# Up-projection's partial sums formed in PSUM: products 6, 7 and 4 added onto product 1, with the pipeline over feature pairs

## The chip, the cores and the metric

One core of one Trainium2 chip runs the whole program in one launch. The core has a matrix engine (PE, TensorE), which multiplies a stationary 128 x 128 weight tile with a moving operand and writes, or adds, the product to an accumulator memory (PSUM, 8 banks of 512 float32 columns over 128 partitions); a vector engine (DVE, VectorE); a scalar engine (ACT, ScalarE); a third one, GpSimd (POOL); and a queue (SP) that issues transfers between the chip's memory and the on-chip buffers. Each engine works through its own list of instructions in order; semaphores make one wait for another. The metric is the time of one execution on the device in microseconds (us), as the median of several runs.

## What is computed

One layer of an encoder: chunked attention and an mLSTM memory side by side, an output projection, and then the feed-forward part, which alone the change touches:

```python
def conv_ffn(h, buf, w_up, w_conv, b_conv, w_down):
    S = h.shape[1]
    u = h @ w_up
    ext = jnp.concatenate([buf.astype(u.dtype), u], axis=1)
    y = b_conv
    for j in range(CONV_W):
        y = y + ext[:, j:j + S] * w_conv[j]
    gate, up = jnp.split(y, 2, axis=-1)
    out = (jax.nn.gelu(gate, approximate=True) * up) @ w_down
    return out, ext[:, S:]
```

There are 2048 prompt tokens and 8 x 16 sample tokens, each of width 1024. `w_up` has 2 x 2816 columns: 2816 for the gate and 2816 for the value `up`; everything is in float32.

## The kernel before

The feed-forward part runs over three blocks of tokens (`FBLOCKS`; 768, 768 and 640 columns). For each block there is an up-projection over 22 features of 128 gate and 128 value columns each, and then a down-projection in two halves. In the profile the up-projections lie at about 1315 to 1645, 1838 to 2150 and 2350 to 2620 us.

**Seven products instead of eight.** For a feature the four results (gate and value, for either half of the block's columns) are a 2 x 2 block product over two halves of the depth, done with seven products in Winograd's form. The moving operands, the seven combinations of the tokens, are `B0` to `B6`, kept in the buffers and made before the block; the weights' sums s1 to s4 are formed on DVE in block 0 (`load_quads`, L1275), stored (`wsd`) and read back in blocks 1 and 2. Each product (`product`) is 12 matmuls into one bank: 4 steps of depth by three terms of a float32 number that is split in a high and a low part (`mm3`, L95 high by high, L96 high by low, L97 low by high). `HALF` is the number of columns of one: 384, 384 and 320. The split of a weight tile takes an ACT cast (L1258) and a DVE subtraction (L1259); seven 128 x 512 tiles a feature.

**The chain of sums.** In the order P1, P6, P7, P5, P2, P4, P3:
- P1 goes to bank `a` (`ua`, from the PSUM tag mm); ACT copies it to x1 (L1481).
- P6 goes to `ub` (tag sm); DVE forms x2 = x1 + P6 (L1483).
- P7 goes to `e`, the first half of `uec` (tag big); DVE forms x3 = x2 + P7 (L1485).
- P5 goes to `c`, the second half of `uec`; DVE adds x3 and c to the second half of the value, uu (`second`, L1411).
- P2 is added onto `a`, and ACT copies it as the first half of the gate, ug (L1498); P4 is added onto `e`, and DVE forms the first half of uu as x2 + e (L1500); P3 is added onto `c`, and DVE adds x2 and c to the second half of ug (L1411).

The profile's buffer names drop numbers, so x1 to x3 all read `x`. Each tag of PSUM has two tiles. x1 to x3 share three slots.

**What follows for a feature.** `conv`: two halo copies on POOL, one ACT step (L1430) and two DVE steps (L1431, L1432) for uu and for ug each, the gelu on ACT (L1434), the product of both on DVE (L1506), and a store to `gd`.

**What sets the order.** `pend` holds the weights two groups ahead (`ahead_of`); a group is the first four (g = 0) or the last three (g = 1) weight tiles of a feature. Split tiles lie in turn in a pair `wh`/`wl` or in four tiles w3. The order in which an engine's instructions stand is set when the program is built: a scheduler simulates the program as written and sorts each engine's queue by it, so that the matmuls of one feature stand among those of its neighbours. On the chip this order is fixed, and each engine waits at its next instruction.

Of the kernel before, what the change touches and what calls it, by code (L numbers as in the profile page):

```python
# [44 lines left out]
def hymba_step(ctx: ExitStack, tc: tile.TileContext, I: dict, O: dict):  # L45
# [981 lines left out]
    P1, P6, P7, P5, P2, P4, P3 = range(7)  # L1027
# [233 lines left out]
    raws = {}  # L1261

    def load_quads(b, f, g):

        src = lambda i: I["w_up"][f][:, i * 512:(i + 1) * 512]
        if b == 0 and g == 0:
            q = []
            for i in range(4):
                q.append(quad(f"wu{f}_{i}"))
                nc.sync.dma_start(q[i], src(i))  # L1270
            a11, a12, a22, a21 = q
            s1, s2, s3, s4 = [quad(f"ws{f}_{i}") for i in range(4)]
            for o, x, y, op in ((s1, a21, a22, ALU.add), (s2, s1, a11, ALU.subtract), (s3, a11, a21, ALU.subtract),
                                (s4, a12, s2, ALU.subtract)):
                nc.vector.tensor_tensor(o, x, y, op=op)  # L1275
            for i, o in enumerate((s2, s3, s1, s4)):
                nc.sync.dma_start(wsd[f][:, i * 512:(i + 1) * 512], o)
            raws[f] = [a12, a22, s4]
            return [a11, s2, s3, s1]
        if b == 0:  # L1280
            return raws.pop(f)
        kept = lambda i: wsd[f][:, i * 512:(i + 1) * 512]
        out = []
        for i, s_ in enumerate([[src(0), kept(0), kept(1), kept(2)], [src(1), src(2), kept(3)]][g]):
            r = quad(f"wu{b}_{f}_{g}_{i}")
            nc.sync.dma_start(r, s_)
            out.append(r)
        return out

    def load_up(b, f, g, quads=None):  # L1290
# [9 lines left out]
        for (h, l), r in zip(at, quads or load_quads(b, f, g)):  # L1300
            split(h, l, r)
        return at
# [73 lines left out]
    p4 = ffn.p4 = ctx.enter_context(tc.tile_pool(name="p4", bufs=1, side="right", reuse_waits="tile"))  # L1376
    pend = [load_up(0, 0, 0)]
# [17 lines left out]
    for b, tiles in enumerate(FBLOCKS):  # L1395
# [70 lines left out]

        def w3_tile(name):
            return p4.tile([P, 1056], F32R, tag="w3", name=name, bufs=4)

        for f in range(NF):  # L1470
# [10 lines left out]
            nc.scalar.copy(x1[:, :n], a[:, :n])  # L1481
# [3 lines left out]
            nc.vector.tensor_tensor(x3[:, :n], x2[:, :n], e[:, :n], op=ALU.add)  # L1485
            product(P5, w[3], c)
# [30 lines left out]
        for dh in range(2):  # L1517
# [7 lines left out]
            if dh == 1:  # L1525
                order = order[2:] + order[:2]
            for c in range(6):
# [5 lines left out]
                elif not last:  # L1533
                    quads = [load_quads(b + 1, 0, i) for i in range(2)]
                    pend = [load_up(b + 1, 0, 0, quads[0])]
# [151 lines left out]
```

## Time and profile before

| what | value |
|---|---|
| time, median of 3 runs | 2800.45 us (2796.61 to 2802.93) |
| profiled execution | 2790.47 us, its span 2788.7 us |
| PE busy | 2725.1 us (98%) |
| DVE busy | 1877.9 us (67%) |
| ACT busy | 1407.6 us (50%) |
| up-projection, block 0: DVE busy in 300 us from 1340 us | 277.8 us |
| up-projection, block 1: DVE busy in 240 us from 1880 us | 190.4 us |

The profile is one execution of its own, so its span is compared with its own time and not with the median. Engines overlap; busy times don't add up to the span. A group of the profile is all instructions of one line, engine, operation and tile, with the mean duration of one. Matmuls overlap in the pipeline: their pace is the distance of two starts and less than the duration of one. In rows of a timeline the first number is the start, the second the duration; what stands in brackets is the engine's idle time before and who ended it.

### The profile page before, as it was taken

To read this page: it belongs to the slowest core of one execution; us is meant where nothing else is said; L and a number is where in the kernel's file an instruction comes from. 1 tells how busy PE (TensorE), PEld (TensorE's weight loads), DVE (VectorE), ACT (ScalarE), POOL (GpSimd) and SP (SyncE) were. 2 spreads that over 40 slices of the span, in tenths; PEclk is the share of its full clock that TensorE was granted. 3 is DMA by queue.
4 is the path that set the end of the run, shared out by engine and by line. 5 is a ranking of instruction groups with operands and counts; after the bars stand their busy time and mean duration, and the time that the engine had idled before them with its cause. 6 is when DMAs were issued, how large, how long until landed. Compare 5 with 4: busy or idle time off the path is not lost.

```text
span 2788.7 us, 47032 instructions
## 1 busy us (share of the span) xinstructions
PE 2725.1 (98%) x16587; PEld 2549.4 (91%) x16587; DVE 1877.9 (67%) x3442; ACT 1407.6 (50%) x2836; POOL 429.0 (15%) x876
## 2 busy tenths in 40 slices
PE   8899999999999999999999999999999999999998
PEld 7899999998899998888999988899999878999887
DVE  5344455656546678666999986468778854888855
ACT  4345545644356666544554555345445543555443
POOL 1000010212100003244211110011111211222211
PEclk9999999999999999999999999999999999999999
DMA  4544355547555455356555455644444774555585
GB/s 165 174 128 126 111 152 160 178 152 219 166 173 148 144 180 172 104 175 227 190 174 167 168 172 174 221 142 156 152 153 151 269 268 146 177 178 175 197 300 188
DMA packets 313418, 486.04 MB, mean 174 GB/s; under 512 B 55426, under 2 KB 150622, under 8 KB 313054
## 3 DMA queue, kind: packets, MB, share of 16 engines
q1 hardware_dynamic: 274590, 449.21, 50.0%
q10 hardware_dynamic: 38592, 33.83, 3.6%
q8 instruction: 130, 2.13, 0.3%
q14 instruction: 106, 0.87, 0.1%
HBM read 359.36 MB, written 126.70 MB: 174 GB/s over the span
## 4 chain that ended last, share of the span: by engine, by line
PE 54%; DVE 3%; DMA 1%; issue 1%; POOL 1%; ACT 1%; SPq 0%; DVEq 0%; POOLq 0%; ACTq 0%
PE uec L95 6%; PE uec L96 6%; PE uec L97 6%; PE dn L97 4%; PE dn L96 3%; PE dn L95 3%; PE ua L97 3%; PE ua L96 3%; PE ua L95 3%; PE dnm L97 2%; PE dnm L95 2%; PE dnm L96 2%; PE wo L97 2%; PE wo L95 2%; PE wo L96 2%; PE ub L97 1%
## 5 line engine op out<-in xcount | busy, mean ns | idle before, releaser
L95 PE MATMUL uec<-B,wuh 128*128 128x384 f32 (+1 forms) x720 | 235.3, 328 | 1.0 <-DVE uu L1411 0.7
L96 PE MATMUL uec<-B,wuh 128*128 128x384 f32 (+1 forms) x720 | 235.4, 327 | 0.0
L97 PE MATMUL uec<-B,wul 128*128 128x384 f32 (+1 forms) x720 | 234.2, 327 | 0.0
L1259 DVE TENSOR_TENSOR gl<-gr,gh 128x768 fp32r<-128x768 f32 (+3 forms) x141 | 121.4, 871 | 153.3 <-ACT gh L1258 137.4
L1258 ACT CAST gh<-gr 128x768 fp32r<-128x768 f32 (+3 forms) x141 | 102.0, 735 | 198.9 <-PE dn L96 174.4
L1258 ACT CAST wuh<-wu 128x512 fp32r<-128x512 f32 x255 | 141.7, 618 | 112.4 <-PE uec L96 100.4
L95 PE MATMUL dn<-wdh,gh 128*128 128x512 f32 x466 | 183.1, 393 | 2.0 <-DVE ug L1411 2.0
L96 PE MATMUL dn<-wdl,gh 128*128 128x512 f32 x466 | 184.0, 395 | 0.0
L97 PE MATMUL dn<-wdh,gl 128*128 128x512 f32 x466 | 168.2, 396 | 0.0
L1259 DVE TENSOR_TENSOR wul<-wu,wuh 128x512 fp32r<-128x512 f32 x255 | 164.9, 685 | 2.8 <-DMA x2d<-mx 2.8
L96 PE MATMUL vo<-wi_l,hT 128*128 128x256 f32 x544 | 155.9, 287 | 0.0
L95 PE MATMUL vo<-wi_h,hT 128*128 128x256 f32 x544 | 155.2, 285 | 0.6 <-DVE mt L199 0.6
L97 PE MATMUL vo<-wi_h,hT 128*128 128x256 f32 x544 | 155.5, 286 | 0.0
L387 DVE CUSTOM_DVE_ANT_0 tmp<-s,nb 128x640 f32<-128x640 f32 (+4 forms) x128 | 94.4, 737 | 80.6 <-PE s L377 74.7
L95 PEld LDWEIGHTS uec<-B,wuh 128*128 128x128 f32 x720 | 135.2, 188 | 3.3 <-DVE uu L1411 1.2
L96 PEld LDWEIGHTS uec<-B,wuh 128*128 128x128 f32 x720 | 135.5, 188 | 0.2
L97 PEld LDWEIGHTS uec<-B,wul 128*128 128x128 f32 x720 | 135.4, 188 | 0.0
L388 ACT ACTIVATE tmp<-tmp,mn 128x640 f32<-128x640 f32 (+4 forms) x128 | 97.6, 762 | 69.5 <-DVE mn L387 65.9
L95 PE MATMUL qk<-hT,wi_h 128*128 128x384 f32 (+1 forms) x384 | 128.4, 334 | 2.9 <-ACT qk_st L226 1.2
L400 DVE TENSOR_TENSOR ptl<-pt,pth 128x640 fp32r<-128x640 f32 (+4 forms) x128 | 93.6, 738 | 55.5 <-ACT pth L399 54.6
L97 PE MATMUL qk<-hT,wi_l 128*128 128x384 f32 (+1 forms) x384 | 128.1, 333 | 0.0
L96 PE MATMUL qk<-hT,wi_h 128*128 128x384 f32 (+1 forms) x384 | 127.8, 333 | 0.0
(411 smaller groups left out, 8875.8 us busy)
## 6 DMA issues: line engine op xcount, KB each, us to landing
wu<-in_w_up SPq DMA_DIRECT2D x220, 256.0 KB, 3.9
wu<-wsd SPq DMA_DIRECT2D x176, 256.0 KB, 3.7
wdr<-in_w_down SPq DMA_DIRECT2D x132, 256.0 KB, 5.0
gr<-gd SPq DMA_DIRECT2D x78, 384.0 KB, 3.1
wi_raw<-in_w_in SPq DMA_DIRECT2D x52, 512.0 KB, 4.0
wsd<-ws SPq DMA_DIRECT2D x88, 256.0 KB, 2.8
gd<-g SPq DMA_DIRECT2D x44, 384.0 KB, 2.4
kraw<-kTd SPq DMA_DIRECT2D x112, 128.0 KB, 3.3
```

What stands on the lines that cost most here:

```text
L95: nc.tensor.matmul(out, ah, bh, start=start, stop=False, skip_group_check=onto)
L96: nc.tensor.matmul(out, ah, bl, start=False, stop=False, skip_group_check=onto)
L97: nc.tensor.matmul(out, al, bh, start=False, stop=stop, skip_group_check=onto)
L387: nc.vector.tensor_tensor_reduce(o_, s_, b_, 1.0, 3e38, ALU.add, ALU.min, accum_out=mn)
L388: nc.scalar.activation(tmp[:, :n], tmp[:, :n], AF.Exp, bias=mn, scale=-1.0, accum_out=rsum[:, i % 4, hh:hh + 1])
L400: nc.vector.tensor_tensor(s.ptl[:, sl, qc], ptv, s.pth[:, sl, qc], op=ALU.subtract)
L1258: nc.scalar.copy(h, r)
L1259: nc.vector.tensor_tensor(l, r, h, op=ALU.subtract)
```

## The change

The seven products are made in the order P1, P5, P6, P2, P7, P4, P3. P6, P7 and P4 are added onto P1 in the same bank `ua`, and ACT copies the running sum out after each: x1 (L1497 or L1520 of the changed kernel), x2 (L1502), x3 (L1507) and the first half of uu (L1522). P5 and then P3 go to `uc` (tag big, one half of it used), P2 to `ud` (tag sm), where DVE adds x1 to it (L1505). `second` is L1424, the convolution L1443 to L1447, the product of gate and value L1528. Three of the five DVE additions of a feature stay, and two ACT copies become four.

P1 of the next feature is issued in this feature's turn, before P4; its weight tile (a11) is therefore loaded (`load_first`) and split with the group before, as the first of g = 1, and the very first of a block on its own (`split_first`). The weights' sums of block 0 are stored in another order, and `late_B` fills the operands of P2, P7, P4 and P3. The rotation of the down-projection's order at dh == 1 is dropped.

```diff
-    P1, P6, P7, P5, P2, P4, P3 = range(7)
+    P1, P5, P6, P2, P7, P4, P3 = range(7)
...
-        for i in (P5, P2, P4, P3):
+        for i in (P2, P7, P4, P3):
...
+    def load_first(b, f):
+
+        firsts[f] = quad(f"wf{b}_{f}")
+        nc.sync.dma_start(firsts[f], I["w_up"][f][:, 0:512])
+        return firsts[f]
...
+        if g:
+            first = [load_first(b, f + 1)] if f < NF - 1 else []
+            return first + (raws.pop(f) if b == 0 else fetched(src(2), kept(3)))
+        if b:
+            return fetched(kept(0), kept(1), src(1), kept(2))
+        a11 = firsts.pop(f)
+        a21, a22, a12 = fetched(src(3), src(2), src(1))
...
+        for i, o in enumerate((s1, s2, s3, s4)):
+            nc.sync.dma_start(wsd[f][:, i * 512:(i + 1) * 512], o)
+        raws[f] = [a22, s4]
+        return [s1, s2, a12, s3]
...
+    def split_first(b, quad_):
+        t = p4.tile([P, 1056], F32R, tag="w3", name=f"wuf{b}", bufs=4)
+        split(t[:, 0:512], t[:, 512:1024], quad_)
+        return t[:, 0:512], t[:, 512:1024]
...
-            a, d_, ec = ps_mm(f"ua{nm}"), ps_sm(f"ub{nm}"), ps_big(f"uec{nm}")
-            e, c = ec[:, 0:512], ec[:, 512:1024]
-            x1, x2, x3 = [p4.tile([P, 384], F32, tag="x", name=f"x{i}_{nm}", bufs=3) for i in range(3)]
-            product(P1, w[0], a)
-            nc.scalar.copy(x1[:, :n], a[:, :n])
-            product(P6, w[1], d_)
-            nc.vector.tensor_tensor(x2[:, :n], x1[:, :n], d_[:, :n], op=ALU.add)
-            product(P7, w[2], e)
-            nc.vector.tensor_tensor(x3[:, :n], x2[:, :n], e[:, :n], op=ALU.add)
-            product(P5, w[3], c)
+            nxt = f"{b}_{f + 1}"
+            if f == 0:
+                a, x1 = ps_mm(f"ua{nm}"), x_tile(f"x1_{nm}")
+                product(P1, first, a)
+                nc.scalar.copy(x1[:, :n], a[:, :n])
+            c, d_, e = ps_big(f"uc{nm}")[:, 0:512], ps_sm(f"ud{nm}"), a
+            product(P5, w[0], c)
+            product(P6, w[1], e, onto=True)
+            x2, x3 = x_tile(f"x2_{nm}"), x_tile(f"x3_{nm}")
+            nc.scalar.copy(x2[:, :n], e[:, :n])
+            product(P2, w[2], d_)
+            ug = u_tile(f"ug{nm}")
+            nc.vector.tensor_tensor(ug[:, 2:2 + n], x1[:, :n], d_[:, :n], op=ALU.add)
+            product(P7, w[3], e, onto=True)
+            nc.scalar.copy(x3[:, :n], e[:, :n])
             uu = u_tile(f"uu{nm}")
             second(uu, x3, c)
             w = pend.pop(0)
...
-            ug = u_tile(f"ug{nm}")
-            product(P2, w[0], a, onto=True)
-            nc.scalar.copy(ug[:, 2:2 + n], a[:, :n])
-            product(P4, w[1], e, onto=True)
-            nc.vector.tensor_tensor(uu[:, 2:2 + n], x2[:, :n], e[:, :n], op=ALU.add)
-            product(P3, w[2], c, onto=True)
+            else:
+                a, x1 = ps_mm(f"ua{nxt}"), x_tile(f"x1_{nxt}")
+                product(P1, w.pop(0), a)
+                nc.scalar.copy(x1[:, :n], a[:, :n])
+            product(P4, w[0], e, onto=True)
+            nc.scalar.copy(uu[:, 2:2 + n], e[:, :n])
+            product(P3, w[1], c, onto=True)
             second(ug, x2, c)
...
             order = list(range(nt))
-            if dh == 1:
-                order = order[2:] + order[:2]
...
+            if dh:
+                first = split_first(b + 1, quads[0])
```

How the queues read with it is shown at two places. In the names the first number is the block, the second the feature, and the last a running number; `B` is numbered by the position of its product in the order. First PE in block 1, feature 4, before: the end of P7 (`B2`), and what comes next, P2 of the same feature (`B4`) and P3 of feature 3 (`B6`).

```order
L95 MATMUL uec1_4_21825<-B2_1_19737,wu31_4_0_1_21657 128x384
L96 MATMUL uec1_4_21825<-B2_1_19737,wu31_4_0_1_21657 128x384
L97 MATMUL uec1_4_21825<-B2_1_19737,wu31_4_0_3_21659 128x384
L95 MATMUL ua1_4_21823<-B4_1_19739,wuh1_4_1_21735 128x384
L96 MATMUL ua1_4_21823<-B4_1_19739,wuh1_4_1_21735 128x384
L97 MATMUL ua1_4_21823<-B4_1_19739,wul1_4_1_21736 128x384
L95 MATMUL uec1_3_21678<-B6_1_19741,wuh1_3_1_21586 128x384
L96 MATMUL uec1_3_21678<-B6_1_19741,wuh1_3_1_21586 128x384
L97 MATMUL uec1_3_21678<-B6_1_19741,wul1_3_1_21587 128x384
```

The products after P7 go to other tiles than the one P7 wrote. PE at the same place of the changed kernel: the end of P7 (now `B4`) and the start of P4 (`B5`).

```order
L95 MATMUL ua1_4_21769<-B4_1_19740,wu31_4_0_1_21678 128x384
L96 MATMUL ua1_4_21769<-B4_1_19740,wu31_4_0_1_21678 128x384
L97 MATMUL ua1_4_21769<-B4_1_19740,wu31_4_0_3_21680 128x384
L95 MATMUL ua1_4_21769<-B5_1_19741,wuh1_4_1_21755 128x384
L96 MATMUL ua1_4_21769<-B5_1_19741,wuh1_4_1_21755 128x384
L97 MATMUL ua1_4_21769<-B5_1_19741,wul1_4_1_21756 128x384
```

P4 now stands directly behind P7, in the same bank, and the copy of x3 has to be made between the two. ACT around that copy, block 1, feature 4 of the changed kernel:

```order
L1502 COPY x2_1_4_21870<-ua1_4_21769 128x384
L1447 ACTIVATE y1_3_0_21818<-y1_3_0_21818 128x768
L1258 CAST wu31_5_1_1_21903<-wu1_5_1_1_21909 128x512
L1507 COPY x3_1_4_21871<-ua1_4_21769 128x384
L1520 COPY x1_1_5_21919<-ua1_5_21918 128x384
L1522 COPY uu1_4_21900<-ua1_4_21769 128x384
```

Between the copies of x2 and x3 stand the gelu of feature 3 and a cast of a weight tile for feature 5, whose slot P7 of feature 4 has read. The same place in block 0, feature 10, where the gelu stands behind the cast:

```order
L1502 COPY x2_0_10_17861<-ua0_10_17750 128x384
L1443 ACTIVATE y0_9_0_17799<-ug0_9_17723,wcv_16243 128x768
L1258 CAST wu30_11_1_1_17894<-ws11_3_17818 128x512
L1447 ACTIVATE y0_9_0_17799<-y0_9_0_17799 128x768
L1507 COPY x3_0_10_17862<-ua0_10_17750 128x384
```

Before, ACT had two copies a feature there, of x1 and of ug, and no copy of P7's bank.

More of the change, by code (lines that the diff above doesn't have):

```diff
@@ L1259, in split @@
         nc.vector.tensor_tensor(l, r, h, op=ALU.subtract)
-    raws = {}
+    raws, firsts = {}, {}
+    def load_first(b, f):
+        firsts[f] = quad(f"wf{b}_{f}")
+        nc.sync.dma_start(firsts[f], I["w_up"][f][:, 0:512])
+        return firsts[f]
     def load_quads(b, f, g):
         src = lambda i: I["w_up"][f][:, i * 512:(i + 1) * 512]
[L1266 to L1281, printed above, removed]
-        kept = lambda i: wsd[f][:, i * 512:(i + 1) * 512]
[L1283 to L1288, printed above, removed]
@@ new lines, in load_quads, with fetched @@
+        kept = lambda i: wsd[f][:, i * 512:(i + 1) * 512]
+        def fetched(*srcs):
+            out = [quad(f"wu{b}_{f}_{g}_{i}") for i in range(len(srcs))]
+            for o, s_ in zip(out, srcs):
+                nc.sync.dma_start(o, s_)
+            return out
+        if g:
[3 more added lines that the diff above has]
+            return fetched(kept(0), kept(1), src(1), kept(2))
@@ L1376, in hymba_step @@
     p4 = ffn.p4 = ctx.enter_context(tc.tile_pool(name="p4", bufs=1, side="right", reuse_waits="tile"))
+    first = split_first(0, load_first(0, 0))
     pend = [load_up(0, 0, 0)]
@@ L1465, in split_g, with x_tile @@
             parts[dh, k] = gh, gl
+        def x_tile(name):
+            return p4.tile([P, 384], F32, tag="x", name=name, bufs=3)
         def w3_tile(name):
@@ L1533, in hymba_step @@
                 elif not last:
-                    quads = [load_quads(b + 1, 0, i) for i in range(2)]
-                    pend = [load_up(b + 1, 0, 0, quads[0])]
+                    quads = [load_first(b + 1, 0)] + [load_quads(b + 1, 0, i) for i in range(2)]
+                    pend = [load_up(b + 1, 0, 0, quads[1])]
                 ks = list(range(4 * c, 4 * c + (4 if c < 5 else 2)))
@@ L1591, in hymba_step @@
                 pass
-            pend.append(load_up(b + 1, 0, 1, quads[1]))
+            pend.append(load_up(b + 1, 0, 1, quads[2]))
     nc.sync.dma_start(O["conv_prompt"], halo)
```

9 lines of the change are left out of this document (7 added, 2 removed).

## The prediction

> **What bounds the kernel now.** I read the page first: the busy times, then the 40 slices.
>
> ```profile
> span 2788.7 us, 47032 instructions
> PE 2725.1 (98%) x16587; PEld 2549.4 (91%) x16587; DVE 1877.9 (67%) x3442; ACT 1407.6 (50%) x2836; POOL 429.0 (15%) x876
> ...
> PEclk9999999999999999999999999999999999999999
> ```
>
> TensorE (PE) is busy for 98% of the span at the full granted clock. The change leaves the number of matmuls in the up-projection as it is, so it can only move the time by PE's idle time. The second view is the table by windows, for the three up-projections (block 0 about 1315 to 1645 us, block 1 about 1838 to 2150, block 2 about 2350 to 2620). Its columns are the window, its length, then busy time and count for PE, PEld, DVE, ACT and POOL, the clock, the DMA share and GB/s.
>
> ```profile
> 1340.00:1400.00 60.00, 58.55 (x335) 57.94 (x334) 55.10 (x86) 30.25 (x48) 15.01 (x16) 1.00 0.62 195
> 1400.00:1460.00 60.00, 59.87 (x344) 59.55 (x343) 56.23 (x88) 30.38 (x51) 10.26 (x16) 1.00 0.50 167
> 1460.00:1520.00 60.00, 59.62 (x339) 58.69 (x339) 54.40 (x84) 30.58 (x49) 9.90 (x16) 1.00 0.50 167
> 1520.00:1580.00 60.00, 59.33 (x340) 58.90 (x340) 55.85 (x85) 29.09 (x47) 11.59 (x16) 1.00 0.52 173
> 1580.00:1640.00 60.00, 59.84 (x344) 59.53 (x343) 56.24 (x88) 32.35 (x53) 10.07 (x18) 1.00 0.50 165
> ...
> 1940.00:2000.00 60.00, 60.00 (x346) 60.00 (x345) 46.86 (x70) 29.50 (x47) 6.98 (x16) 1.00 0.49 155
> ...
> 2480.00:2540.00 60.00, 60.00 (x412) 60.00 (x411) 54.07 (x110) 34.49 (x60) 13.39 (x40) 1.00 0.55 177
> ```
>
> Blocks 1 and 2 have no PE idle time at all; nothing can be won there. Block 0 has a little: VectorE (DVE) is busy 93% of the time there (277.8 of 300 us), since it also forms the weight sums, and PE loses 2.8 us by its busy time, or, against some 346.8 matmuls per window at block 1's pace, 32 matmuls of 0.173 us = 5.5 us. **So the most that the change can win here is 5.5 us, and it can lose wherever PE now waits.**
>
> **What the change adds: a read between two products of one bank.** Before, P1 goes to `ua`, P6 to `ub`, P7 to half of `uec`, and nothing accumulates onto P6 or P7 until their sums have long been read. Now P6, P7 and P4 go onto P1's bank, and each partial sum is copied out by ACT before the next product may start. Where the other feature's products stand between, the copy is free. The order of the changed kernel shows where they do not: in every third feature (4, 7, ..., 19 of each block, 18 places) P4 follows P7 directly, and in feature 0 of block 2. The price of such a place comes from these rows of block 1: the last two matmuls of P1 and the next product's first, the copy that waits for P1, and a wait of PE for a DVE split.
>
> ```profile
> 1907.31 0.34 PE L96 MATMUL ua<-B,wuh 128*128 128x384 f32 x1
> ...
> 1907.48 0.34 PE L97 MATMUL ua<-B,wul 128*128 128x384 f32 x1
> ...
> 1907.65 0.34 PE L97 MATMUL ub<-B,wul 128*128 128x384 f32 x1
> ...
> 1907.85 0.48 ACT L1481 COPY x<-ua 128x384 f32<-128x384 f32 x1 [2.00 <-PE ua L97]
> ```
> ```profile
> 1332.86 1.28 DVE L1259 TENSOR_TENSOR wul<-wu,wuh 128x512 fp32r<-128x512 f32 x2
> ...
> 1333.59 0.45 PE L97 MATMUL ua<-B,wul 128*128 128x384 f32 x1 [1.59 <-DVE wul L1259]
> ...
> 1333.87 0.34 PE L95 MATMUL ua<-B,wuh 128*128 128x384 f32 x1
> ```
>
> A matmul starts every 0.173 us and takes 0.34; its reader starts 0.03 us after its end (1907.82 to 1907.85). Of the two splits in the second fence the first ends at about 1333.55 (0.69 us, below), PE starts 0.04 later, and its next matmul comes 0.28 us after, 0.11 more than the pace: 0.15 us from a release to full pace. Behind the waiting product stand all of PE's later ones, and the other engines' work waits for those, so that a stall is paid in full. A bare copy between two products therefore costs 0.34 + 0.03 + 0.48 + 0.15 - 0.173 = **0.83 us**.
>
> The copy isn't alone. In ACT's queue a weight cast (L1258 before) stands ahead of it whose target tile P7 itself has just read, so that the cast can't start before P7's last L96 matmul, and in block 0 the gelu (L1434 before) stands between. Their prices (the groups of lines 1340 to 2620 us, block 2's copy, four casts in a row, and block 2's matmuls):
>
> ```profile
> L1258 ACT CAST wuh<-wu 128x512 fp32r<-128x512 f32 x250 | 138.8, 617 | 110.2 <-PE uec L96 98.2 <-issue 11.3 <-DMA wu<-in_w_up 0.6
> ...
> L1434 ACT ACTIVATE y<-y 128x768 f32<-128x768 f32 x44 | 37.3, 848 | 71.0 <-DVE y L1432 71.0
> ...
> L1481 ACT COPY x<-ua 128x384 f32<-128x384 f32 x42 | 20.1, 479 | 31.4 <-PE ua L97 31.3
> ```
> ```profile
> L1481 ACT COPY x<-ua 128x320 f32<-128x320 f32 x19 | 8.0, 423 | 8.8 <-PE ua L97 8.8
> ```
> ```profile
> 1901.57 2.18 ACT L1258 CAST wuh<-wu 128x512 fp32r<-128x512 f32 x4 [3.56 <-PE uec L96]
> ```
> ```profile
> 2405.02 0.31 PE L97 MATMUL ua<-B,wul 128*128 128x320 f32 x1
> 2405.16 0.31 PE L95 MATMUL ua<-B,wuh 128*128 128x320 f32 x1
> ```
>
> Four casts in a row take 2.18 us, so each but the last takes 0.52. With t = 0 at the start of P7's last matmul, L96 ends at 0.17.
> - Block 1, one cast and the copy: 0.17 + 0.03 + 0.52 + 0.48 + 0.15 = 1.35, less 0.173 = 1.18 us; 6 places, **7.1 us**.
> - Block 0, the gelu too: 1.18 + 0.85 = 2.0 us; 6 places, **12.2 us**. The gelu needs the second convolution step (L1432 before); by DVE's order one addition, six splits, three weight sums of the same size and two convolution steps lie between P3's end and that step's (0.55 + 9 x 0.69 + 2 x 1.02 = 8.8 us, rows below), and PE has 53 matmuls, 9.2 us, in that time: I take it as ready.
> - Block 2, matmuls of 0.31 at a pace of 0.147, copy 0.42: 0.16 + 0.03 + 0.52 + 0.42 + 0.15 - 0.147 = 1.13 us; 6 places, **6.8 us**. Its feature 0 has three casts ahead: 0.16 + 0.03 + 1.56 + 0.42 + 0.15 - 0.147 = **2.2 us**. Block 1's feature 0 has three casts and two matmuls between: 0.17 + 0.03 + 1.56 + 0.48 + 0.15 - 3 x 0.173 = **1.9 us**.
> - In features 2, 5, ..., 17 of block 1 ten matmuls of P2 stand between and three casts ahead: 2.39 - 11 x 0.173 = 0.5 us, six times, and 2.32 - 11 x 0.147 = 0.7 in block 2's feature 2: **3.7 us**.
> - The last feature has the x2 copy directly between P6 and P7 in blocks 0 and 2 (0.83 and 0.77), and after it the down-projection's first matmuls wait for their weights' casts, which stand behind the copies; I take 1 us for each block. This stretch had idle time of its own, 1.7, 0.6 and 5.3 us in the three windows below, part of which is the same wait; I set 3 us against it: **+1.6 us**.
>
> ```profile
> 1640.00:1700.00 60.00, 58.26 (x269) 47.34 (x268) 41.72 (x58) 34.41 (x58) 3.91 (x11) 1.00 0.58 194
> 2120.00:2180.00 60.00, 59.44 (x312) 54.71 (x311) 46.50 (x68) 31.98 (x54) 8.97 (x19) 1.00 0.45 147
> 2600.00:2660.00 60.00, 54.68 (x279) 47.32 (x278) 47.35 (x84) 28.36 (x50) 16.49 (x23) 0.97 0.71 246
> ```
>
> All other places where a product waits for a copy have 18 or more matmuls between (3.1 us at 0.173), which covers a copy and three casts (0.03 + 1.56 + 0.48).
>
> **What it removes.** Five DVE additions per feature become three, and two ACT copies become four.
>
> ```profile
> L1259 DVE TENSOR_TENSOR wul<-wu,wuh 128x512 fp32r<-128x512 f32 x250 | 161.6, 685 | 0.0
> ...
> L1432 DVE SCALAR_TENSOR_TENSOR y<-ug,wcv,y 128x768 f32<-128x768 f32 x44 | 44.7, 1015 | 0.1
> ...
> L1485 DVE TENSOR_TENSOR x<-x,uec 128x384 f32<-128x384 f32 x42 | 23.2, 552 | 11.3 <-PE uec L97 11.2
> ```
>
> DVE loses 2 x 0.55 us of some 13.5 us per feature in block 0 (93% of 14.5 us), so falls to about 87%; ACT gains 2 x 0.48 on 7.4 (30.5 of 60 us) and stays below 60%. Of block 0's 2.8 to 5.5 us I give back **4 us**. Outside block 0 no PE time hangs on DVE. The same seven weight loads and four stores are issued per feature, in another order; late_B handles four products as before; the dropped rotation of the down-projection's order and the early split of the first weight lie where PE is fully busy (the window 1820 to 1840 has 20.00 of 20), so I cost them at nothing; if that cover were gone, a late split is 0.62 + 0.69 us per block.
>
> ```profile
> 1820.00:1840.00 20.00, 20.00 (x94) 17.02 (x93) 11.52 (x18) 9.58 (x19) 1.00 (x3) 1.00 0.41 131
> ```
>
> **The sum.** 12.2 + 7.1 + 6.8 + 2.2 + 1.9 + 3.7 + 1.6 = 35.5 us, less 4 = **+31 us**. The profiled execution took 2790.5 us (span 2788.7), so about 2821 for its like; the median of the runs shown is 2800.45, 10 us above it, so **2831 us**. What the trace cannot show is ACT's order at run time with PE late: from below, every direct place at the bare 0.83 us (0.77 in block 2), 12 x 0.83 + 7 x 0.77 + 0.5 (block 1's feature 0) + 1.6 = 17.5 us, less the full 5.5, is +12; from above, one late DVE step of 1.0 us (L1432 takes about that) at each of the 18 places more is +49. I stand nearer the middle, since the cast ahead of the copy is fixed in ACT's queue.
>
> **Rivals.** (a) *Bare copies*: casts run earlier than I think, or DVE's relief is worth all 5.5 us: +12 us, 2812. For it: ACT is half idle. Against it: the cast waits for P7's own matmul, so an idle ACT doesn't help.
> (b) *DVE is late at the direct places*: the gelu or the conv ahead of the copy waits for L1432, as it does now for 71.0 us in all, and PE waits behind it: +49 us, 2850. For it: 8.8 us of DVE work in 9.2. Against it: each stall of PE gives DVE time to catch up.
> (c) *Faster: DVE in block 0 was the only limit that counts.* Then block 0 runs at block 1's pace and the direct places cost nothing: 5.5 us won, less 1.6: 2796. For it: DVE's 93%. It decides below 5.5 / 20, about 0.3 us for a place; against it stands the 0.48 us of the copy alone. The Trainium skill (Perfetto Trace Analysis, Optimizing Scalar/DVE Operations) speaks for this rival: with a saturated DVE, moving work to ScalarE may pay. The same page (Optimizing Tensor Performance, Matmuls) speaks against the change: independent matmul groups should rotate through PSUM banks so that a read overlaps the next group, and the direct places do the opposite. The trace of before agrees with the second in that PE never idles in block 1; the first it bears out in block 0 alone.
> (d) *No change*: most stalls are covered by what I don't see, and +12 less 8 us of block ends leaves 2804.
> (e) *The granted clock falls* because of the short stalls. If it stood at the 0.97 of the window at 2600 us through the three up-projections (330 + 312 + 270 us), 3% or 27 us more: 2858. Against it: that window had 5.3 us idle in 60, after the changes block 1 would have about 1.4; and the stretch around the wait of 1.59 us (1316 to 1340 us) stands at 1.00:
>
> ```profile
> 1316.00:1340.00 24.00, 21.86 (x123) 20.97 (x123) 23.20 (x30) 14.74 (x22) 6.13 (x5) 1.00 0.69 248
> ```
>
> The Trainium skill (TensorE: Matmul & The Clock Gate, A second HAM failure mode: psum-queue depth-cycling) tells of a kernel whose clock swung between half and full because PE idled briefly between matmul groups; the rows of this case show nothing of that kind at stalls of this length.
>
> **How the numbers follow.** Forecast 0.60, bare copies 0.12, late DVE 0.13, clock 0.03, faster 0.07, no change 0.05. The forecast alone spans 2820 to 2842 (its terms of 1.1 to 2.0 us by a fifth, and 4 us of spread of the median). The range goes from 2808, just under (a), to 2850, (b). A measurement of this kernel can tell about 0.2% (5.6 us) from no change; by that bound faster is 0.08 (c and a little of d), same 0.07, slower 0.85.
>
> **What would show it.** In the profile after, block 1's windows should show 58 to 59 of 60 us of PE busy instead of 60.00; the waits of PE should list matmuls of `ua` on the ACT copy of x3 (about 20 of them, some 0.2 us less than the prices above, since the list counts from a matmul's end and not the slow restart), and these copies should show a PE release followed by a cast just ahead. Block 0's count per window should fall by the stalls (one of 2 us in 43 us of features). If x3 waits in block 0 are near 0.8 us, the gelu wasn't ahead; if they are over 2.5, DVE was late. If block 1's windows stay at 60.00, the step that is wrong is that a copy between two products on one bank can't be hidden.

## The result, and the profile after

The changed kernel takes 2834.51 us (median of 4 runs, 2831.88 to 2835.29); the kernel before, beside it on the same chip, 2799.3 us. The ratio is 1.0121, with a 95% interval of 1.0109 to 1.0133: slower by 35 us, or 1.2%. The profiled execution took 2834.05 us, its span 2832.3 us.

The page of the changed kernel, span and busy times first:

```profile
span 2832.3 us, 46944 instructions
PE 2740.8 (97%) x16587; PEld 2551.9 (90%) x16587; DVE 1823.0 (64%) x3310; ACT 1458.7 (52%) x2968; POOL 415.3 (15%) x876
```

The same 16587 matmuls; DVE has 132 instructions less and 55 us less work, ACT 132 more and 51 us more. PE's share fell. The windows of the three up-projections, with the columns of the table of before:

```profile
1400.00:1460.00 60.00, 56.72 (x324) 56.08 (x323) 49.02 (x72) 31.28 (x54) 6.70 (x16) 1.00 0.49 158
1460.00:1520.00 60.00, 58.36 (x335) 58.04 (x334) 50.66 (x76) 33.03 (x56) 6.22 (x14) 1.00 0.52 169
...
1940.00:2000.00 60.00, 58.65 (x333) 57.70 (x333) 42.90 (x61) 33.35 (x59) 4.43 (x14) 1.00 0.52 158
2000.00:2060.00 60.00, 58.87 (x336) 58.23 (x335) 42.19 (x60) 32.83 (x57) 6.15 (x18) 1.00 0.46 141
2480.00:2540.00 60.00, 58.23 (x395) 57.70 (x395) 47.98 (x95) 36.76 (x69) 12.63 (x37) 1.00 0.58 174
```

Blocks 1 and 2, which had 60.00 of 60 us before, now have 58.2 to 58.9; block 0 went from 59.3 to 59.9 down to 56.7 to 58.4, although DVE is less busy there (49 to 52 us in the windows from 1400 us on, instead of 54 to 56). The waits of PE say for whom it idles (line waited for, total, times, longest):

```profile
PE ua L95 <- ACT x L1507: 25.9, 27, 1.9
PE dnm L95 <- ACT gh L1258: 3.4, 1, 3.4
PE ud L96 <- DVE B L1146: 2.2, 1, 2.2
```

One wait holds 25.9 us: the next product onto `ua` waits for ACT's copy of x3 (L1507). One row of each kind, in order of time: the start of block 0, block 0's steady state (six of 1.64 us), block 1's feature 0, its places with ten matmuls of P2 between P7 and P4 (six of 0.22), its direct places (six of 0.92), block 2's feature 0, and block 2's direct places (six of 0.89). The 27th is 0.46 us in block 2's feature 2.

```profile
1334.55 0.44 PE L96 MATMUL ud<-B,wuh 128*128 128x384 f32 x1 [2.20 <-DVE B L1146]
...
1405.45 0.44 PE L95 MATMUL ua<-B,wuh 128*128 128x384 f32 x1 [1.64 <-ACT x L1507]
...
1871.93 0.44 PE L95 MATMUL ua<-B,wuh 128*128 128x384 f32 x1 [1.59 <-ACT x L1507]
1901.68 0.44 PE L95 MATMUL ua<-B,wu 128*128 128x384 f32 x1 [0.22 <-ACT x L1507]
1932.22 0.45 PE L95 MATMUL ua<-B,wuh 128*128 128x384 f32 x1 [0.92 <-ACT x L1507]
...
2396.50 0.42 PE L95 MATMUL ua<-B,wuh 128*128 128x320 f32 x1 [1.93 <-ACT x L1507]
...
2449.13 0.41 PE L95 MATMUL ua<-B,wuh 128*128 128x320 f32 x1 [0.89 <-ACT x L1507]
```

And ACT's and PE's rows at the first wait of 1.64 us:

```profile
1403.67 0.62 ACT L1258 CAST wu<-ws 128x512 fp32r<-128x512 f32 x1 [4.35 <-PE ua L96]
1404.19 0.84 ACT L1447 ACTIVATE y<-y 128x768 f32<-128x768 f32 x1
1404.94 0.46 ACT L1507 COPY x<-ua 128x384 f32<-128x384 f32 x1
```
```profile
1403.47 0.34 PE L97 MATMUL ua<-B,wu 128*128 128x384 f32 x1
1405.45 0.44 PE L95 MATMUL ua<-B,wuh 128*128 128x384 f32 x1 [1.64 <-ACT x L1507]
1405.73 0.34 PE L96 MATMUL ua<-B,wuh 128*128 128x384 f32 x1
```

ACT had been idle for 4.35 us when PE's last L96 matmul of P7 set the cast's slot free; then the cast, the gelu and the copy ran one behind the other. The matmul behind starts 1.98 us after the last one (the pace is 0.173) and the next 0.28 us later, so that the place costs 1.98 - 0.173 + 0.28 - 0.173 = 1.91 us: the listed wait and 0.27 us more. By the same working a place costs 1.18 us in block 1 and 1.16 in block 2.

**By blocks.** The spans of two executions also differ in the part ahead of the feed-forward, so the kernels are compared from the first matmul of a block's up-projection to that of the next (block 2: to the end of the span). Before, these lie at 1315.47, 1836.25 and 2349.33 us, after at 1320.64, 1853.44 and 2380.33.

| kernel | median us | block 0 | block 1 | block 2 |
|---|---|---|---|---|
| before | 2799.3 | 520.8 | 513.1 | 439.4 |
| after | 2834.5 | 532.8 | 526.9 | 451.9 |
| before, once more | 2798.4 (one run) | 521.3 | 512.5 | 439.5 |
| P4 behind P6 | 2823.5 | 533.8 | 519.4 | 445.0 |
| copy ahead of cast | 2827.4 | 528.2 | 524.7 | 452.0 |
| second copy | 2851.7 | 544.0 | 528.7 | 452.3 |
| P4 behind P6, late weights | 2817.3 | 530.2 | 516.3 | 442.3 |
| P6 between P7 and P4 | 2828.6 | 530.9 | 527.8 | 443.1 |
| the same, start mended | 2823.7 | 525.4 | 528.0 | 444.0 |
| P4 behind P6 from feature 2 | 2809.6 | 526.6 | 515.2 | 441.6 |

The three blocks lost 12.0, 13.8 and 12.6 us, together 38.4. The medians are of all executions, the blocks of the profiled one alone. The other 5.2 us between the two spans lie ahead of 1320 us. They are no part of the change: the kernel before, profiled once more, began its feed-forward at 1323.51 us instead of 1315.47, with block times within 0.6 us of the first.

### The profile page after: what moved, and what is told of

It reads as the page before. It is cut to its first block, busy times and chain, and to the rows that moved or that the text cites. A ratio compares the mean times of both kernels' runs of the same rounds, so it can differ in the third digit from the quotient of the medians.

```text
span 2832.3 us, 46944 instructions
## 1 busy us (share of the span) xinstructions
PE 2740.8 (97%) x16587; PEld 2551.9 (90%) x16587; DVE 1823.0 (64%) x3310; ACT 1458.7 (52%) x2968; POOL 415.3 (15%) x876
## 5 line engine op out<-in xcount | busy, mean ns | idle before, releaser
L95 PE MATMUL ua<-B,wuh 128*128 128x384 f32 (+1 forms) x708 | 234.4, 331 | 25.5 <-ACT x L1507 24.2
L97 PE MATMUL ua<-B,wul 128*128 128x384 f32 (+1 forms) x708 | 232.1, 328 | 0.8 <-DVE wul L1259 0.8
L96 PE MATMUL ua<-B,wuh 128*128 128x384 f32 (+1 forms) x708 | 232.1, 328 | 0.0
L95 PE MATMUL dn<-wdh,gh 128*128 128x512 f32 x466 | 185.0, 397 | 0.9 <-DVE ug L1424 0.9
L96 PE MATMUL dn<-wdl,gh 128*128 128x512 f32 x466 | 184.4, 396 | 0.0
L95 PEld LDWEIGHTS ua<-B,wuh 128*128 128x128 f32 x708 | 133.3, 188 | 32.5 <-ACT x L1507 30.1
L96 PE MATMUL vo<-wi_l,hT 128*128 128x256 f32 x544 | 155.7, 286 | 0.0
L1258 ACT CAST wuh<-wu 128x512 fp32r<-128x512 f32 x210 | 118.2, 617 | 37.8 <-PE uc L96 36.2
L1444 DVE SCALAR_TENSOR_TENSOR y<-uu,wcv,y 128x768 f32<-128x768 f32 (+1 forms) x66 | 64.6, 978 | 109.4 <-ACT y L1443 76.2
L97 PEld LDWEIGHTS ua<-B,wul 128*128 128x128 f32 x708 | 133.5, 189 | 1.1 <-DVE wul L1259 1.1
L1259 DVE TENSOR_TENSOR wul<-wu,wuh 128x512 fp32r<-128x512 f32 x210 | 134.2, 685 | 0.1
L96 PEld LDWEIGHTS ua<-B,wuh 128*128 128x128 f32 x708 | 133.6, 189 | 0.1
L95 PE MATMUL qk<-hT,wi_h 128*128 128x384 f32 (+1 forms) x384 | 128.7, 335 | 1.3 <-DVE gates L273 0.7
```

Of the source, the lines that this page charges most:

```text
L95: nc.tensor.matmul(out, ah, bh, start=start, stop=False, skip_group_check=onto)
L96: nc.tensor.matmul(out, ah, bl, start=False, stop=False, skip_group_check=onto)
L97: nc.tensor.matmul(out, al, bh, start=False, stop=stop, skip_group_check=onto)
L1258: nc.scalar.copy(h, r)
L1259: nc.vector.tensor_tensor(l, r, h, op=ALU.subtract)
L1444: nc.vector.scalar_tensor_tensor(y[:, :ln], u[:, 1:1 + ln], w_(1), y[:, :ln], op0=ALU.mult, op1=ALU.add)
```

## The experiments

The theory is the prediction's: PE idles because a copy has to be made between two products onto one bank, and it idles for as long as ACT needs for what stands ahead of the copy and for the copy. Rivals: the accumulation costs something in itself, or PE waits for DVE's chain. In the edits `product` returns its first and last matmul, `behind(later, earlier)` puts one instruction after another in its engine's queue (an order, no semaphore), `read` is the copy of x3, and `tc.issue_after(read.ins)` puts what follows behind it.

**One: P4 of the feature before behind P6 of this one.** This takes P4 away from P7's heels and changes nothing else of the work.

```diff
-            product(P6, w[1], e, onto=True)
+            m6 = product(P6, w[1], e, onto=True)
+            if f:
+                behind(held, m6[1])
...
-            product(P4, w[0], e, onto=True)
+            held = product(P4, w[0], e, onto=True)[0]
```

> The changed kernel with one added order on PE: the first matmul of P4 of a feature is issued behind the last one of P6 of the next feature, so that 14 or more matmuls stand between P7 and P4 of one bank everywhere but in a block's last feature (2 matmuls there, four casts ahead of the copy of x3). Same matmuls, copies, casts and additions. Theory (the lost time is PE's wait for the copy of x3 where P4 follows P7 directly, or too soon): the 27 waits of matmuls of ua on the copy of x3 go, that is 6 x 1.9 us in block 0, 6 x 1.2 + 7 x 0.5 + 1.9 in block 1, 6 x 1.2 + 2.2 + 1.5 (clock) + 0.7 in block 2, some 35 us together; the last features pay 2.4 us each, 1.5 more if the clock drops, together 7 to 12: about 2807 us, and block 1's windows show 60.00 of 60 us. Rival 1 (the price is ACT's larger load, or the new order of loads and products): nothing goes, 2830 to 2835. Rival 2 (a read of a bank between two products that add to it costs PE by itself, whatever stands between): at most half goes, about 2820.

Measured: 2823.47 us (2822.96 to 2827.61), against 2802.02 of the kernel before beside it: 1.0080 (1.0067 to 1.0093). It won 11 us of the 35, some 16 less than expected; the time alone would fit the second rival as well (about 2820), but the windows don't. In blocks 1 and 2 from feature 2 on, 23 to 25 matmuls now stand between P1 and P6 and between P6 and P7, 47 or 48 between P7 and P4, and the x3 waits are gone but for a block's last feature, where only two matmuls stand between P7 and P4. The windows in these blocks:

```profile
1940.00:2000.00 60.00, 60.00 (x346) 60.00 (x345) 44.08 (x65) 34.56 (x60) 9.30 (x16) 1.00 0.49 151
2060.00:2120.00 60.00, 60.00 (x346) 60.00 (x345) 41.78 (x60) 33.78 (x58) 10.21 (x17) 1.00 0.45 142
2480.00:2540.00 60.00, 60.00 (x412) 60.00 (x411) 48.21 (x99) 38.41 (x70) 19.01 (x40) 1.00 0.59 174
```

60.00 of 60 us, with the counts of before (346 and 412): where enough stands between, the accumulation costs nothing in itself. The miss lies elsewhere, in new waits that the forced order made:

```profile
PE uc L95 <- DVE uu L1431: 4.8, 5, 1.5
PE ua L95 <- ACT x L1529: 4.2, 2, 2.3
PE ua L95 <- ACT x L1516: 3.5, 3, 1.2
...
PE ud L96 <- DVE B L1147: 2.2, 1, 2.2
PE uc L95 <- DVE ug L1431: 1.7, 1, 1.7
```

In block 0 products onto `uc` wait for DVE's addition that reads P5's sum; in blocks 1 and 2 feature 1's P6 waits about 2 us for the copy of x1 (L1529), and in all three blocks the last feature's P4 about 1.2 us for that of x3 (L1516).

**Two: the copy ahead of the cast.** At the direct places the order on PE stays as in the changed kernel; on ACT the copy goes first.

```diff
+            if f % 3 == 1 and f > 1:
+                behind(gelus[f - 1], read)
+                with tc.issue_after(read.ins):
+                    ahead_of(2 * f + 3)
+            else:
+                ahead_of(2 * f + 3)
```

> The changed kernel with the order of PE kept at the 18 direct places (features 4, 7, ..., 19: P5 and P2 of the next feature, then P7, then P4), and ACT's order changed there: the copy of x3 stands ahead of the weight cast and of the gelu that stood ahead of it. Theory (the price is the whole chain on ACT between P7 and P4): the listed wait falls from 1.64 (block 0), 0.92 (block 1) and 0.89 us (block 2) to 0.55, 0.55 and 0.5 us at each, worth 6 x 1.1 + 6 x 0.37 + 6 x 0.36 = 11 us; in block 0, and by less in block 2, the features after them now have three casts ahead at ten matmuls, 0.5 us each, 5 x 0.5 + 5 x 0.15 = 3 us back: about 2826 us. Rival (what stands ahead of the copy doesn't matter, PE waits for something else): waits and time stay, 2834.

Measured: 2827.36 us, 1.0092 (1.0078 to 1.0106). The first direct place in block 0 and the first in block 2:

```profile
1409.97 0.44 PE L95 MATMUL ua<-B,wuh 128*128 128x384 f32 x1 [0.57 <-ACT x L1519]
...
2447.20 0.41 PE L95 MATMUL ua<-B,wuh 128*128 128x320 f32 x1 [0.51 <-ACT x L1519]
```

All twelve direct waits of blocks 0 and 1 fell to 0.57 us, those of block 2 to 0.51 or 0.52. With the 0.27 us of overhead that is 0.84 us a place, the 0.83 that the prediction had worked out for a bare copy. So what stands ahead of the copy on ACT is 1.07 us of block 0's 1.64 and 0.35 of block 1's 0.92. The time fell by 7 us, about as expected: block 0 gained 4.6 us and not 6.4, since five places there now have ten matmuls between P7 and P4 and wait 0.22 us each.

Block 2 looks like an exception, as its waits fell by 2.2 us and its block time didn't. From its first matmul to its last, its up-projection did get shorter, from 288.1 to 286.3 us. What followed got longer by as much, from 163.8 to 165.7 us: there PE waits 3.3 us (3.4 in the changed kernel), and the granted clock stood at half for 6.8 us instead of 3.4. Two windows behind this wait, first of this run, then of the changed kernel (the seventh number, ahead of the DMA share, is the clock):

```profile
2687.00:2693.00 6.00, 6.00 (x15) 4.69 (x15) 3.55 (x5) 1.06 (x2) 3.92 (x3) 0.52 1.05 402
2690.00:2696.00 6.00, 6.00 (x21) 4.74 (x20) 4.03 (x6) 1.46 (x2) 4.01 (x3) 0.72 1.05 401
```

So the gain at the copies was there, and it was lost behind the up-projection, for the most part by the clock.

**Three: a second copy.** P7's bank is copied twice, the first time to a tile that nobody reads; ACT's order stays.

```diff
+            if f % 3 == 1 and f > 1:
+                nc.scalar.copy(junk[:, :n], e[:, :n])
+            read = nc.scalar.copy(x3[:, :n], e[:, :n])
```

> The changed kernel with its own orders kept on PE and ACT, and one more copy of the sum (128 x 384 or 128 x 320, to a tile that nobody reads) on ACT just ahead of the copy of x3 at the 18 direct places. Theory (the whole chain on ACT is paid there): each wait is longer by one copy, 0.38 to 0.42 us: 1.64 becomes 2.04, 0.92 becomes 1.32, 0.89 becomes 1.25; that alone is +7 us, 2841. In the changed kernel two waits of 1.93 and 2.20 us were followed by some 3.4 us at clock 0.50, and waits of 1.64 us were not. Theory A (an idle time of 1.9 us or more takes the clock down): the six places of block 0 lose another 1.5 us each, +16 us in all, 2850. Theory B (those two had another cause): no stretch at 0.50 behind the waits of 2.04, 2841. Rival (ACT's copies are covered): no change, 2834.

Measured: 2851.7 us, 1.0178 (1.0164 to 1.0192), about as expected. The waits grew by 0.38 us in blocks 0 and 1 (to 2.02 and 1.30) and by 0.32 in block 2, which is one copy each in a row of copies. In block 0 the price was far more than that: it took 11 us more than the changed kernel's, for 6 x 0.38 = 2.3 us. The windows that begin 0.15 to 0.7 us after the restart from each of the six waits of 2.02 us tell why:

```profile
1411.00:1414.00 3.00, 3.00 (x11) 3.00 (x10) 1.43 (x3) 0.03 (x1) 0.18 (x1) 0.50 0.56 218
1459.00:1462.00 3.00, 3.00 (x11) 3.00 (x11) 1.23 (x3) 0.00 (x0) 0.18 (x1) 0.50 0.57 218
1507.00:1510.00 3.00, 3.00 (x11) 3.00 (x10) 1.03 (x3) 0.00 (x0) 0.18 (x1) 0.50 0.56 218
1555.00:1558.00 3.00, 3.00 (x19) 3.00 (x18) 1.34 (x3) 0.89 (x2) 0.18 (x1) 1.00 0.57 218
1601.00:1604.00 3.00, 3.00 (x13) 3.00 (x14) 1.58 (x4) 0.18 (x1) 0.18 (x1) 0.70 0.57 218
1649.00:1652.00 3.00, 3.00 (x14) 3.00 (x13) 0.79 (x2) 0.09 (x1) 0.18 (x1) 0.66 0.56 211
```

After five of the six the granted clock went to half for a while, and 11 to 14 matmuls ran in 3 us, against 19 after the fourth, where it stayed. At some 1.5 us for each fall (worked out in the last section) the five and the 2.3 us make about 10 of the 11. PE is called busy all the while; only the clock and the count show it.

**Four: as one, and the casts behind the copy in the last feature.** The weights of the down-projection that are cast in feature 21 go behind x3's copy.

```diff
             if f < NF - 1:
                 ahead_of(2 * f + 2)
...
+                with tc.issue_after(read.ins):
+                    ahead_of(2 * f + 2)
```

> As the first of this group, and in a block's last feature the first weights of the down-projection are cast behind the copy of x3, so that the copy follows P7 at once. Theory: 4 to 10 us less than the first of this group, since three waits of 2 us or more become 0.5 to 0.6 us: about 2800 us, that is, the time before the change. Rival (the first weights of the down-projection, now later, are missed there): no gain, 2807.

Measured: 2817.28 us, 1.0051 (1.0038 to 1.0064): 6 us better than one, and 17 over what was expected of it. What was left stands in PE's rows of this kernel: the start of block 0, one of five waits there for DVE's addition, and feature 1 of blocks 1 and 2.

```profile
1341.76 0.44 PE L96 MATMUL ud<-B,wuh 128*128 128x384 f32 x1 [2.20 <-DVE B L1147]
...
1629.77 0.45 PE L95 MATMUL uc<-B,wuh 128*128 128x384 f32 x1 [1.81 <-DVE uu L1431]
...
1876.48 0.44 PE L95 MATMUL ua<-B,wu 128*128 128x384 f32 x1 [1.97 <-ACT x L1532]
...
2390.40 0.63 PE L95 MATMUL ua<-B,wu 128*128 128x320 f32 x1 [2.25 <-ACT x L1532]
```

**Five: less order.** Only P4 of the features 4, 7, 10 and so on (and of feature 1 in blocks 1 and 2) goes behind the next feature's P6, and feature 0's second group of casts in blocks 1 and 2 goes behind the copy of x3.

```diff
+            if f % 3 == 2 and (f > 2 or b):
+                behind(held, m6[1])
...
+            if b and f == 0:
+                with tc.issue_after(read.ins):
+                    ahead_of(2 * f + 3)
```

> The changed kernel with P4 put behind the next feature's P6 only where P4 stood directly behind P7 (features 4, 7, ..., 19, and feature 1 of blocks 1 and 2), and in feature 0 of blocks 1 and 2 the casts of the second weight group put behind the copy of x3. Sums, banks, copies and additions are those of the changed kernel. Theory (nothing but the order loses the time): of the 35 us go 11.5 + 7.1 + 7.0 at the direct places, 1.4 and 2.9 in the features 0 (the second with its stretch at half clock), and some 3 at the places with ten matmuls: 2801 us, the time before the change, with block 1's windows at 60.00 of 60 us. Rival (the accumulation itself, with four copies on ACT and three reads in a row of one bank, costs time wherever it stands; the 15 us that the first group left are its price): 2815 us.

Measured: 2828.56 us, 1.0103 (1.0087 to 1.0119), some 27 us above the expectation. In block 0 five waits for DVE's addition (0.78 to 1.71 us) came in. In block 1 P6 of the next feature now stands directly behind P7, its twelve matmuls between P7 and P4, and the wait moved to P6 itself. ACT and then PE there:

```profile
1932.67 0.62 ACT L1259 CAST wu<-wu 128x512 fp32r<-128x512 f32 x1 [1.98 <-PE ua L96]
1933.19 0.47 ACT L1516 COPY x<-ua 128x384 f32<-128x384 f32 x1
1933.56 0.48 ACT L1533 COPY x<-ua 128x384 f32<-128x384 f32 x1
```
```profile
1934.10 0.44 PE L95 MATMUL ua<-B,wuh 128*128 128x384 f32 x1 [1.30 <-ACT x L1533]
```

P6 is added onto the next feature's P1, whose copy of x1 (L1533) stands on ACT behind the cast and the copy of x3: 0.92 us and one more copy, 0.38. That P1 was long done, with 36 matmuls between it and P6; its copy stood behind a cast that P7 had only just set free. So it isn't distance to P1 that P6 lacks: it waits for ACT's queue. In block 2, where 24 matmuls came to stand between P7 and the next P6, there was no such wait from feature 2 on (60.00 of 60 us in both windows from 2480 to 2600 us).

**Six: as five, and the start of block 0 mended.** Feature 1's weight sums and splits go behind the split of P2's operand on DVE.

```diff
+            if b == 0 and f == 0:
+                with tc.issue_after(ffn.late.ins):
+                    ahead_of(2 * f + 2)
```

> As the fifth run, and at the start of block 0 the weight sums and splits of feature 1 stand behind the split of P2's operand on DVE, for which PE waits 2.2 us in the changed kernel, followed by 3.4 us at clock 0.50. Theory: 2.2 + 1.5 us less than the fifth run, about 2797 us, 0.1% faster than before the change, since block 0 then keeps what DVE's relief is worth. Rival (DVE is full there, and the work put back is missed a little later): same as the fifth run, 2801.

Measured: 2823.65 us, 1.0081 (1.0067 to 1.0095). Against five, beside it, that is 5 us less; the wait for P2's operand fell from 2.2 to 0.7 us, and block 0 from 530.9 to 525.4. That is the gain that was expected; the 27 us that five had missed stayed.

**Seven: the kernel before, once more.**

> The kernel before the change, unchanged, for a second profile of it. In the first one the up-projection starts at 1315.5 us, in the changed kernels at 1320 to 1327 us, though the change lies behind that. Theory (the part ahead differs from execution to execution): the second profile starts it some us later, with the same 336.8, 329.2 and 277.8 us for the three up-projections. Rival (the change moves that part too): it starts at 1315 to 1316 again.

One run of 2798.38 us; its blocks stand in the table above. The windows and blocks of before repeat, and the part ahead of the feed-forward doesn't.

**Eight: what had worked, together.** P4 behind P6 from feature 2 on, the late weights of four, the casts of five, and the start of six.

```diff
+            if f > 1:
+                behind(held, m6[1])
```

> The change with its accumulation and its pairs kept; the order of issue is pinned as in e4 (product 4 of the feature before behind product 6) from feature 2 of every block on, so that feature 1's product 6 isn't put ahead of its operand; feature 21's down weights, and in blocks 1 and 2 feature 0's second group of weight casts, stand behind the third copy on ScalarE; in block 0 feature 1's weight sums and splits stand behind the split of product 2's operand on VectorE. Theory (what e4 had left was feature 1's wait in blocks 1 and 2, the late operand at the start and VectorE's late weight pieces in block 0): block 0 about 526, block 1 about 514, block 2 about 439, so about 2806 us, within 0.4% of the kernel before. Rival (the waits of e4 in block 0 belong to the pairs' demand on VectorE and don't go by an order of issue): block 0 stays at 530 and the time at about 2812 to 2815.

Measured: 2809.63 us (2807.05 to 2812.66), 1.0032 (1.0021 to 1.0044). Block 0 came out at 526.6, where the theory had 526; blocks 1 and 2 at 515.2 and 441.6, 1.2 and 2.6 above it; the time is between the two expectations. Its windows in block 0, 1 and 2:

```profile
1460.00:1520.00 60.00, 59.32 (x340) 59.00 (x339) 50.81 (x76) 32.83 (x57) 12.59 (x16) 1.00 0.50 159
1520.00:1580.00 60.00, 58.89 (x337) 58.25 (x335) 51.23 (x77) 33.75 (x59) 10.68 (x15) 1.00 0.55 175
...
1940.00:2000.00 60.00, 60.00 (x346) 60.00 (x345) 44.39 (x65) 34.93 (x61) 13.99 (x17) 1.00 0.53 161
2480.00:2540.00 60.00, 60.00 (x411) 60.00 (x410) 49.78 (x101) 37.89 (x71) 22.47 (x40) 1.00 0.64 188
```

So by order alone 25 of the 35 us come back, with the accumulation, the four copies and the pairs all kept. What is left in block 0 is of another kind. The timeline of one such place:

```profile
1444.38 0.69 DVE L1293 TENSOR_TENSOR ws<-wu,wu 128x512 f32<-128x512 f32 x1 [0.60 <-DMA wu<-in_w_up]
...
1444.98 0.55 DVE L1433 TENSOR_TENSOR uu<-x,uc 128x384 f32<-128x384 f32 x1
...
1445.59 0.44 PE L95 MATMUL uc<-B,wuh 128*128 128x384 f32 x1 [0.71 <-DVE uu L1433]
```

The next product onto `uc` waits for the addition that reads it (L1433), and that stands on DVE behind a weight sum, which had itself waited 0.60 us for its weights. It is again a reader behind other work in its engine's queue, now on DVE: the copy of x3 that it adds had been made over 6 us earlier (ACT, 1437.90 us). To put the addition ahead of the sum wasn't tried. No version was found that beats the kernel before.

## Why the prediction held

The mechanism was the one predicted, and its terms can be set beside what they measured (a listed wait and 0.27 us):

| term | predicted us | measured us |
|---|---|---|
| block 0, six direct places | 6 x 2.0 = 12.2 | 6 x 1.91 = 11.5 |
| block 1, six direct places | 6 x 1.18 = 7.1 | 6 x 1.18 = 7.1 |
| block 2, six direct places | 6 x 1.13 = 6.8 | 6 x 1.16 = 7.0 |
| feature 0 of blocks 2 and 1 | 2.2 + 1.9 | 2.2 + 1.86 |
| ten matmuls between | 3.7 | 6 x 0.49 + 0.73 = 3.7 |
| ends of the blocks | +1.6 | about 0 |
| DVE's relief in block 0 | -4 | -3.7 |
| start of block 0 | 0 | +2.9, and 1.5 by the clock |
| clock after feature 0 of block 2 | 0 | +1.5 |
| sum | +31 | +35.6 |

- **The gelu ahead of the copy in block 0.** The prediction took the gelu as ready, not waiting for DVE. All six waits are 1.64 us, and the gelu starts as the cast lets it; experiment two took cast and gelu away and left 0.57. Rival (b), DVE late, would have shown waits over 2.5 us.
- **Bare copies**, rival (a), is what experiment two built: 0.84 us a place. In the changed kernel the cast was ahead in every queue, as its order says.
- **Faster**, rival (c): DVE's relief was real. The waits of the kernel before between 1340 and 1640 us, 1.39, 0.38, 0.68 and 0.16 us, are gone; with 0.27 us for each that is 3.7 us, and DVE's share there fell to 85% (254.3 of 300 us; the prediction's own figures, 1.1 us off 13.5 in 14.5, give that too, and not its 87%). It was a ninth of what the copies cost (33 us).
- **The start of block 0 costed at nothing** is a step that failed. P2 is now the fourth product instead of the fifth, and its operand's split on DVE came 2.20 us late; the five waits of that start add up to 4.2 us, against 2.15 in two before (0.56 and 1.59), and with 0.27 us for each the difference is 2.9 us. Experiment six confirmed the place. The prediction had looked only at the window at 1820 us, where another block starts.
- **The clock**, rival (e), was right in kind and not in size: in the up-projections it fell at two places, for some 3.4 us each, and not throughout.
- **The ends of the blocks** cost nothing on balance: the waits there add up to 7.2 us after and 7.4 before. The sentence that all other places have 18 or more matmuls between is not quite right (block 0's features 0 and 1 have 10 between P7 and P4, its feature 0 has 14 between P1 and P6, block 2's last 11 between P7 and P4), but of these only P6 of block 0's feature 0 waited, for 0.27 us.
- **The down-projection costed at nothing** is the other step that failed. The measured terms add up to 35.6 us and the blocks to 38.4, and the rest lies there: from the last matmul of an up-projection to the next block (or the end) it takes 185.0, 184.8 and 163.3 us before and 185.4, 187.4 and 163.8 after. Its matmuls start every 0.231 us on average in both profiles of the kernel before and every 0.232 to 0.233 in all eight of the changed kernels (intervals under 0.3 us), which over 2244 of them is some 3 us. The change that touches this part, the dropped rotation of its order, was in all eight. No run put it back, so the cause stays open.

So the blocks lost 7 us more than the +31 of the sum. That the median (2834.5 us) came within 4 us of the forecast's 2831 is in part luck: the part ahead of the feed-forward differs from execution to execution. In the changed kernel's profile (2834.05 us) it ended 3 us earlier than in the second profile of the kernel before (2798.38 us), at 1320.6 instead of 1323.5 us, and so hid 3 of the 38 us.

The Trainium skill (Perfetto Trace Analysis, Matmuls) says that independent groups of matmuls should rotate through the banks, so that a read overlaps the next group. Blocks 1 and 2 of the experiments one and eight agree: with 23 to 25 matmuls of other banks (some 4.2 us at a pace of 0.173) between two products onto one bank, the read between them cost nothing. Experiment five shows that the distance of the two products isn't all: with 36 matmuls between them PE still waited 1.30 us, because the read stood behind work that had just been set free. What has to be long enough is the stretch from the last product that anything in the queue up to the read waits for.

## What to carry to other kernels

- Accumulation in PSUM saves additions, but a partial sum that has to be read between two products makes a chain of product, read, product. What it costs is not the length of the read but the whole queue ahead of the read on the engine that makes it (here 0.84 us bare, 1.18 with a cast ahead, 1.91 with a cast and a gelu), less the matmuls of other banks that stand between, counted from the product that sets the queue going.
- When a wait is ordered away, look at what now follows it: the copies behind it in the same queue can hold up the next product, as in experiment five, and the expectation of a clean profile is an upper bound of the gain.

## What the hardware showed that was not expected

The granted clock fell after idle times of PE of about 2 us. Three windows of the changed kernel, beginning about 0.5 us after the restart from waits of 2.20, 1.64 and 1.93 us:

```profile
1335.00:1338.00 3.00, 3.00 (x12) 3.00 (x12) 3.00 (x3) 0.00 (x0) 0.00 (x0) 0.59 1.01 404
...
1406.00:1409.00 3.00, 3.00 (x19) 3.00 (x18) 1.55 (x4) 1.05 (x2) 0.18 (x1) 1.00 0.57 218
2397.00:2400.00 3.00, 3.00 (x14) 3.00 (x13) 0.94 (x5) 0.34 (x1) 0.38 (x2) 0.51 0.79 240
```

For some 3.4 us the matmuls then came every 0.32 us instead of 0.174 (0.267 instead of 0.147 in block 2), which loses 3.4 x (1 - 0.174 / 0.32) = 1.5 us, nearly as much again as the wait. Counted over the feed-forward parts of all ten profiles, none of the waits of 1.48 to 1.89 us was followed by it, and 25 of 31 waits of 1.93 us and more were: all three of 1.93, five of seven of 2.02, seven of eight of 2.18 to 2.25. The six that were not are 1.97, 1.98, 2.02 twice, 2.21 and 3.02 us long. So the length alone doesn't decide above 1.9 us.

The trace's record of the granted clock shows what else does. In one execution all falls and rises lie a whole number of 3.413 us apart: in the changed kernel at 1335.52, 1338.93, 2397.06 and 2400.48 us, and 2397.06 - 1335.52 is 311 x 3.413. These marks cut the time into equal stretches, and a wait that lies across a mark is split by it. The longest piece of each wait separates the two kinds without an exception: at most 1.81 us in all the waits that weren't followed by a fall (the one of 3.02 us is 1.25 and 1.77, that of 2.21 is 1.79 and 0.42), at least 1.93 us in the 25 that were. One more fall, in the first experiment at 1662.24 us, followed two waits of 0.53 and 1.20 us within one stretch, so the idle time of a stretch seems to add up and the border isn't sharp. Where the marks lie differs from execution to execution, so that a wait of 2 us can cost 2 us or 3.5.

The Trainium skill (TensorE: Matmul & The Clock Gate, What's actually happening) states a free-running window of 3.4 us after which the clock halves when PE was idle in it. The marks and the length of the slow stretch agree with that (twice it was two stretches, 6.8 us, in the experiments two and six). That a whole window has to be idle does not, since 1.93 us within one were enough; here the measurement decides.
